# A transformer layer's down-projection in two halves of K, 27 of its 44 weight pieces by seven block products instead of eight

## The chip, the core and the metric

The kernel runs on one core of a Trainium2 chip. A core has a matrix engine (TensorE; PE for its matmuls, PEld for its weight loads), VectorE (DVE), ScalarE (ACT), GpSimd (POOL) and SyncE (SP), each with an instruction queue of its own that runs in order, 16 DMA engines that all queues share, an on-chip memory of 128 partitions and eight accumulation banks of 128 x 512 fp32. The metric is the device time of one execution in microseconds (us).

## What is computed

One layer on 256 tokens of width 2048, all fp32: a mixer (8 attention heads with a forget gate beside 8 HGRN2 heads), cross-attention into 256 memory tokens, and a gated convolutional FFN, each followed by a residual sum and a LayerNorm. The part that the change rewrites is the last product of the FFN:

```python
def conv_ffn(x, w_up, conv_w, conv_b, w_down):
    h = x @ w_up                      # 2048 -> 2 * 5632
    h = causal_depthwise_conv(h, conv_w) + conv_b      # width 3
    a, b = jnp.split(h, 2, axis=-1)
    return (jax.nn.silu(a) * b) @ w_down               # 5632 -> 2048
...
x = layer_norm(DEEPNORM_ALPHA * x + ff, ln3_g, ln3_b)
```

The part that sits early in the program and matters here is `hgrn2_chunkwise`: products of forget gates over ever larger blocks of tokens (prefix products `pre`, suffix products `suf`), which scale queries and keys.

## The kernel before, in words

**Precision.** Every big product splits both operands into a high fp32r part and a low one (`split`, L76: ACT casts the high part, L77; DVE subtracts, L78) and adds three products: high x high, high x low, low x high.

**Weights.** A slot of the program uses one or more loads. A load (`Load`, L88) is one 1 MB DMA of 128 x 2048 fp32 on SP's queue (L99) into one of three `raw` buffers (`RAW_BUFS`), then two `split`s of 128 x 1024 each. `advance` (L154) keeps loads and splits `ahead` loads in front of the slot. All split weights, activations and other work tiles come from one pool of 38 units (`unit`, 4 KB a partition).

**Order of the program.** `run` (L165) walks the slots. In each it pumps one step of the oldest background task (`pump`), runs what was deferred to this slot (`later`), and then the slot's matmuls. Slots of the first 200 us are projections of the mixer (`product_ft`, 16 + 16 matmuls a slot; `product_tok`, 24 a slot). The HGRN2 work (`hgrn`) runs beside them as a background task, twice (g = 0, 1). The instructions of each engine are then put in order by a scheduler, at build time; only dependences on data and the edges that `hold` (L70) draws bind it.

**POOL's part.** For each g `hgrn` has POOL set a quarter of `suf` to one (L463) and clear `AT` (L495). DVE reads that quarter in the reciprocal of L484, and writes into `AT` by a predicated copy in L508. `forget_weights` clears two `ffw` tiles on POOL (L615), into which ACT and DVE put the forget gate's weights (L77, L78). Later POOL issues three DMAs (L657, L660) through a scratch in DRAM, and does five of the splits ahead of the up-projection.

**Down-projection.** `block_output(aps["down"], 11, gT, ...)` (L1081): four blocks of 512 columns, for each 11 pieces of 512 rows of K. A piece is a slot: for both halves t of the tokens, four K steps of three 128 x 512 matmuls (`tok_steps`, L266 to L268), 24 in all. The last four pieces run in one slot, token half by token half, so that the first half's LayerNorm lies under the second half's matmuls. It begins after the whole up-projection, whose gated result stays in 22 tiles `gT`.

## Time and profile before

| | |
|---|---|
| time, median of 3 runs | 1578.58 us (1578.27 to 4043.96) |
| the profiled execution's own time | 1578.25 us |
| its span | 1576.5 us |
| PE busy | 1560.5 us, 99% of the span |
| PEld, DVE, ACT, POOL busy | 85%, 65%, 49%, 1% |
| DMA | 299.29 MB, 190 GB/s over the span |
| down-projection's matmuls | 1324.2 to 1563.6 us, 1056 of 128 x 512 |

Times in the rows are us from the span's start unless marked ns. A matmul's own duration (390 ns) is longer than the distance from one to the next, since they are pipelined. PEld overlaps PE. A view by stretches gives each engine's busy time (with its count of instructions), the granted TensorE clock as a share of full speed, the mean busy share of the 16 DMA engines and the bytes that they moved per second. In the rows "<-" names what is read, behind what is written; in brackets or behind a bar stands the idle time ahead of an instruction and what ended it.

### The profile page before, as it was taken

The page shows a single profiled execution, that of the slowest core. Times are in us where ns is not written, and L with a number is a line of the kernel's source. Part 1 is how long each engine was busy: PE and PEld are TensorE (multiplying, and loading weights), DVE is VectorE, ACT ScalarE, POOL GpSimd, SP SyncE. Part 2 cuts the span into 40 slices and gives each one's busy share as a digit, 9 for nine tenths or more (in the row PEclk, how much of TensorE's full clock was granted, in tenths as well). Part 3 has the DMA queues.
Part 4 walks back from the last instruction along what each step waited for, and adds up shares of the span by engine and source line. Part 5 has one row for each costly group of instructions (what it writes and reads, how often), then busy time and mean ns, then how long its engine had stood idle before and what let it go on. Part 6 is the DMA issues. An engine that isn't in the chain of part 4 may idle for free.

```text
span 1576.5 us, 20804 instructions
## 1 busy us (share of the span) xinstructions
PE 1560.5 (99%) x8324; PEld 1347.3 (85%) x8324; DVE 1025.7 (65%) x1444; ACT 772.2 (49%) x1128; POOL 10.9 (1%) x24
## 2 busy tenths in 40 slices
PE   9999999999999999999999999999999999999996
PEld 7888888888888888988889888888888888888885
DVE  6567468667764775555747976776777777454464
ACT  5453354455553344444617655565555556433340
POOL 0000000000000000000000000000000000000000
PEclk9999999999999999999999999999999999999998
DMA  8565255455445545444733754544454456556551
GB/s 308 193 231 223 109 197 183 175 226 195 155 186 215 212 162 185 161 161 173 271 144 121 275 195 186 214 187 168 180 187 172 176 187 224 202 188 215 195 204 54
DMA packets 45793, 299.29 MB, mean 190 GB/s; under 512 B 5368, under 2 KB 5760, under 8 KB 11264
## 3 DMA queue, kind: packets, MB, share of 16 engines
q1 hardware_dynamic: 45376, 296.90, 51.1%
q8 instruction: 65, 1.06, 0.3%
q0 software_dynamic: 320, 1.06, 0.2%
q14 instruction: 32, 0.26, 0.0%
HBM read 295.83 MB, written 2.11 MB: 189 GB/s over the span
## 4 chain that ended last, share of the span: by engine, by line
PE 98%; DVE 1%; DMA 0%; issue 0%; SPq 0%; DVEq 0%; ACT 0%
PE acc L204 35%; PE acc L206 18%; PE acc L266 13%; PE acc L267 13%; PE acc L268 13%; PE xs L913 1%; PE xo L943 1%; PE lev L536 1%; PE acc L215 0%; PE acc L222 0%; DMA xraw<-in_xT_dram 0%; PE ntr L848 0%; PE fo L760 0%; PE ffacc L623 0%; PE lev L502 0%; PE ho L578 0%
## 5 line engine op out<-in xcount | busy, mean ns | idle before, releaser
L78 DVE TENSOR_TENSOR wlo<-raw,whi 128x1024 fp32r<-128x1024 f32 (+1 forms) x540 | 642.3, 1213 | 262.9 <-ACT whi L77 229.4
L77 ACT CAST whi<-raw 128x1024 fp32r<-128x1024 f32 (+1 forms) x540 | 547.5, 1044 | 277.0 <-PE acc L267 180.9
L204 PE MATMUL acc<-act,whi 128*128 128x512 f32 x2384 | 572.9, 392 | 1.8 <-DVE act L78 1.6
L204 PEld LDWEIGHTS acc<-act,whi 128*128 128x128 f32 x2384 | 438.3, 188 | 87.9 <-DVE act L78 2.0
L206 PEld LDWEIGHTS acc<-act,wlo 128*128 128x128 f32 x2384 | 307.3, 192 | 12.3
L266 PE MATMUL acc<-whi,act 128*128 128x512 f32 x800 | 312.7, 391 | 0.0
L268 PE MATMUL acc<-whi,act 128*128 128x512 f32 x800 | 311.4, 389 | 0.0
L267 PE MATMUL acc<-wlo,act 128*128 128x512 f32 x800 | 311.3, 389 | 0.0
L206 PE MATMUL acc<-act,wlo 128*128 128x256 f32 x2384 | 310.9, 283 | 0.0
L268 PEld LDWEIGHTS acc<-whi,act 128*128 128x128 f32 x800 | 150.2, 188 | 31.4
L266 PEld LDWEIGHTS acc<-whi,act 128*128 128x128 f32 x800 | 150.2, 188 | 30.6
L267 PEld LDWEIGHTS acc<-wlo,act 128*128 128x128 f32 x800 | 150.2, 188 | 30.4
L226 ACT COPY half<-acc 128x256 f32<-128x256 f32 x144 | 53.5, 371 | 144.9 <-PE acc L206 139.4
L959 ACT ACTIVATE cy<-hbuf,convp 128x256 f32<-128x256 f32 x88 | 52.8, 600 | 39.3 <-DVE hbuf L227 39.3
L960 DVE SCALAR_TENSOR_TENSOR cy<-hbuf,convp,cy 128x256 f32<-128x256 f32 x88 | 42.3, 482 | 26.5 <-ACT cy L959 26.5
L77 ACT CAST act<-cy 128x256 fp32r<-128x256 f32 x76 | 30.8, 406 | 57.8 <-DVE cy L978 37.6
L227 DVE TENSOR_TENSOR hbuf<-acc,half 128x256 f32<-128x256 f32 x88 | 36.9, 421 | 29.0 <-ACT half L226 28.3
L266 PE MATMUL acc<-whi,mixT 128*128 128x512 f32 x128 | 50.0, 390 | 0.0
L268 PE MATMUL acc<-whi,mixT 128*128 128x512 f32 x128 | 49.8, 389 | 0.0
L267 PE MATMUL acc<-wlo,mixT 128*128 128x512 f32 x128 | 49.8, 389 | 0.0
L770 DVE SCALAR_TENSOR_TENSOR res<-res,acc 128x512 f32<-128x512 f32 x24 | 16.4, 685 | 48.2 <-PE acc L268 48.2
L78 DVE TENSOR_TENSOR act<-cy,act 128x256 fp32r<-128x256 f32 x76 | 32.0, 422 | 18.7 <-ACT act L77 18.5
(204 smaller groups left out, 723.2 us busy)
## 6 DMA issues: line engine op xcount, KB each, us to landing
raw<-in_up_dram SPq DMA_DIRECT2D x88, 1024.0 KB, 4.8
raw<-in_down_dram SPq DMA_DIRECT2D x44, 1024.0 KB, 4.8
raw<-in_w_ws_dram SPq DMA_DIRECT2D x29, 1024.0 KB, 4.9
raw<-in_w_xs_dram SPq DMA_DIRECT2D x24, 1024.0 KB, 4.9
raw<-in_xk_dram SPq DMA_DIRECT2D x16, 1024.0 KB, 4.9
raw<-in_w_out_dram SPq DMA_DIRECT2D x16, 1024.0 KB, 4.9
raw<-in_xv_dram SPq DMA_DIRECT2D x16, 1024.0 KB, 4.8
raw<-in_xq_dram SPq DMA_DIRECT2D x16, 1024.0 KB, 4.8
```

The costliest lines, as they stand in the source:

```text
L77: nc.scalar.copy(hi, src)
L78: engine.tensor_tensor(lo, src, hi.bitcast(F32), op=ALU.subtract)
L204: nc.tensor.matmul(acc, lhsT=hi, rhs=flat(x), start=k == 0, stop=False)
L206: nc.tensor.matmul(acc[:, 0:S], lhsT=lo, rhs=x[:, 0], start=False, stop=k == KD - 1)
L226: nc.scalar.copy(half, acc[:, S:2 * S])
L227: nc.vector.tensor_tensor(dst, acc[:, 0:S], half, op=ALU.add)
L266: nc.tensor.matmul(acc[t], lhsT=x[:, 0, ts], rhs=hi[:, cols], start=first and j == 0, stop=False)
L267: nc.tensor.matmul(acc[t], lhsT=x[:, 0, ts], rhs=lo[:, cols], start=False, stop=False)
L268: nc.tensor.matmul(acc[t], lhsT=x[:, 1, ts], rhs=hi[:, cols], start=False, stop=last and j == 3)
L770: nc.vector.scalar_tensor_tensor(z, in0=z, scalar=ALPHA, in1=acc, op0=ALU.mult, op1=ALU.add)
L959: nc.scalar.activation(y, h[:, 2:S + 2], AF.Identity, bias=convp[:, 3, f:f + 1], scale=convp[:, 2, f:f + 1])
L960: nc.vector.scalar_tensor_tensor(y, in0=h[:, 1:S + 1], scalar=convp[:, 1, f:f + 1], in1=y, op0=ALU.mult, op1=ALU.add)
```

## The change

**Two halves.** The first 22 feature blocks of the up-projection are followed by the down-projection of their half of K, then comes the second half of both. Each half of the down-projection is 2 x 11 pieces: 2 blocks of 1024 columns, 11 pieces of 256 rows of K. A piece is still 1 MB, now as four blocks of 128 x 512, and still one slot or part of the last one.

**Seven products.** For 27 of the 44 pieces (6 and 6 in the first half, 8 and 7 in the second) the eight block products (2 token halves x 2 K steps x 2 column blocks, three matmuls each) become seven, after Strassen (Winograd's form). Such a piece reads three of its four blocks (768 KB) and a second load of four sums of its blocks (1 MB), and uses four sums of activation blocks, made by `gate_sums` on DVE and split (14 pairs of feature blocks). Its products go to seven accumulators, four of which are combined by `early` after the last such piece of a group of 11; the others take the remaining pieces' eight products too.

**Weight sums.** The four sums of a piece are made in DRAM by six DMAs on POOL's queue (`weight_sums`): a copy of one block to two places, an adding DMA of 128 x 1024 on both, and twice a copy of 128 x 512 and an adding DMA on it. 27 pieces need 162 DMAs, listed in groups of four pieces, step by step. `make_sums` takes one of them off the list in each slot from 72 on, behind a copy of one column on DVE and one on POOL (`marks`).

**Elsewhere.** `ahead` is 2 through the whole up-projection (it was 1 from f = 34 on and in the down-projection).

```diff
+HALVES = 2
+PAIRS = NF // 2 // HALVES
+SEVEN = ((6, 6), (8, 7))
+
+SUMS_FROM = 72
...
+        def __init__(self, src, into=None, cols=2048):
...
+            if self.cols % 1024:
+                w = unit([P, 2, 512], F32R, name="wone")
+                split(w[:, 0], w[:, 1], self.raw[:, 0:512])
+                self.halves.append((w[:, 0], w[:, 1]))
+            for c in range(self.cols % 1024, self.cols, 1024):
                 hi = unit([P, 1024], F32R, name="whi")
                 lo = unit([P, 1024], F32R, name="wlo")
-                split(hi, lo, self.raw[:, h * 1024:(h + 1) * 1024])
+                split(hi, lo, self.raw[:, c:c + 1024])
                 self.halves.append((hi, lo))
+
...
+    class LaterLoad(Load):
+        def dma(self, pieces=1):
+            self.src = self.src()
+            super().dma(pieces)
...
+                make_sums(mine[0].halves[0][0][:, 0:1].bitcast(F32))
                 body(*[m.halves for m in mine])
...
+    def weight_sums(keys, src):
+        def ops(key):
+            w = src(key)
+            t = dp.tile([P, 2048], F32, name=f"wsum{len(made)}")
+            made[key] = t
+            pool = nc.gpsimd
+            yield lambda: pool.dma_start(r3(t[:, 0:1024], 2), w[:, 0:512].unsqueeze(1).broadcast_to((P, 2, 512)))
+            yield lambda: pool.dma_start(t[:, 0:1024], w[:, 512:1536], accum_op=ALU.add)
+            yield lambda: pool.dma_start(t[:, 1024:1536], t[:, 512:1024])
+            yield lambda: pool.dma_start(t[:, 1024:1536], w[:, 512:1024], accum_op=ALU.add)
+            yield lambda: pool.dma_start(t[:, 1536:2048], t[:, 1024:1536])
+            yield lambda: pool.dma_start(t[:, 1536:2048], w[:, 1536:2048], accum_op=ALU.add)
+        for i in range(0, len(keys), 4):
+            for step in zip(*[list(ops(k)) for k in keys[i:i + 4]]):
+                sums_to_make.extend(step)
+    def make_sums(seen):
+        if sums_to_make and state["slot"] >= SUMS_FROM:
+            i = len(sums_to_make) % 8
+            nc.vector.tensor_copy(marks[:, i:i + 1], seen)
+            nc.gpsimd.tensor_copy(marks[:, 8 + i:9 + i], marks[:, i:i + 1])
+            sums_to_make.pop(0)()
+    def three(acc, x, w, start, stop):
+        nc.tensor.matmul(acc, lhsT=x[0], rhs=w[0], start=start, stop=False)
+        nc.tensor.matmul(acc, lhsT=x[0], rhs=w[1], start=False, stop=False)
+        nc.tensor.matmul(acc, lhsT=x[1], rhs=w[0], start=False, stop=stop)
...
+    def columns_1024(pieces, sums, act, act_sums, seven, evac_early, evac, stagger):
+        rest = [i for i in range(len(pieces)) if i not in seven]
+        order, free = [], len(rest) - stagger
+        for n, i in enumerate(seven):
+            order += [i] + rest[n * free // len(seven):(n + 1) * free // len(seven)]
+        order += rest[free:]
+        one, two = {}, {}
+        def into(d, key, tag):
+            start = key not in d
+            if start:
+                d[key] = bank("acc", tag)
+            return d[key], start
+        def seven_body(i):
+            def body(ws, ts):
+                w11, (w22, w21) = ws[0], (block_of(ws[1], 0), block_of(ws[1], 1))
+                (t1, t3), (t2, t4) = ([block_of(t, j) for j in range(2)] for t in ts)
+                x, s = act[i], [(act_sums[i][:, 0, j], act_sums[i][:, 1, j]) for j in range(4)]
+                stop = i == seven[-1]
+                for key, a, b in ((1, x_of(x, 0, 0), w11), (5, s[0], t1), (6, s[1], t2), (7, s[2], t3)):
+                    acc, start = into(one, key, "m")
+                    three(acc, a, b, start, stop)
+                for key, a, b in ((2, x_of(x, 0, 1), w21), (3, s[3], w22), (4, x_of(x, 1, 1), t4)):
+                    acc, start = into(two, key, "g")
+                    three(acc, a, b, start, False)
+            return body
+        def eight(ws, i, t, h, stop):
+            acc, start = into(two, ((2, 3), (4, 8))[t][h], "g")
+            for kk in range(2):
+                three(acc, x_of(act[i], t, kk), block_of(ws[kk], 1 - h), start and kk == 0, stop and kk == 1)
+        def eight_body(i):
+            def body(ws):
+                for t in range(2):
+                    for h in range(2):
+                        eight(ws, i, t, h, False)
+            return body
+        def last_body(*wss):
+            ends = order[-stagger:]
+            for t in range(2):
+                for h in range(2):
+                    for i, ws in zip(ends, wss):
+                        eight(ws, i, t, h, i == ends[-1])
+                    evac(t, h, two[((2, 3), (4, 8))[t][h]])
+        for i in order[:-stagger]:
+            if i in seven:
+                slot([Load(pieces[i][:, 512:2048], cols=1536), LaterLoad(sums[i])], seven_body(i),
+                     (lambda: evac_early(one)) if i == seven[-1] else None)
+            else:
+                slot([pieces[i]], eight_body(i))
+        slot([pieces[i] for i in order[-stagger:]], last_body)
...
     def ffn_b(f):
         def done(y):
+            p = f // 2
             if f % 2 == 0:
                 gT.append(unit([P, 2, 2, S], F32R, name="act"))
-            nc.vector.tensor_tensor(y, gate[f], y, op=ALU.mult)
-            split(gT[f // 2][:, f % 2, 0], gT[f // 2][:, f % 2, 1], y)
+                if p % PAIRS < max(SEVEN[p // PAIRS]):
+                    gated[p] = unit([P, 4, S], name="gated")
+            if p in gated:
+                z = gated[p][:, f % 2]
+            else:
+                z = y
+            nc.vector.tensor_tensor(z, gate[f], y, op=ALU.mult)
+            split(gT[p][:, f % 2, 0], gT[p][:, f % 2, 1], z)
+            if p in gated and f % 2:
+                later(lambda: gate_sums(p))
         return lambda acc: conv(NF + f, acc, done)
+
+    def gate_sums(p):
+        x = gated[p]
+        s = x[:, 2:4].rearrange("p a (b c) -> p (a b) c", b=2)
+        x11, x21, x12, x22 = (x[:, k, t * P:t * P + P] for k in range(2) for t in range(2))
+        for o, a, b, op in ((0, x21, x22, ALU.subtract), (2, x11, x21, ALU.subtract),
+                            (1, s[:, 0], x11, ALU.subtract), (3, x12, s[:, 1], ALU.add)):
+            nc.vector.tensor_tensor(s[:, o], a, b, op=op)
+        gS[p] = unit([P, 2, 4, P], F32R, name="sums")
+        split(gS[p][:, 0], gS[p][:, 1], s)
...
-    set_ahead(2)
-    for f in range(1, NF):
-        if f > 1:
-            product_ft(aps["up"][f], x2T, ffn_a(f))
-        product_ft(aps["up"][NF + f], x2T, ffn_b(f))
-        if f == 34:
-            set_ahead(1)
-    set_ahead(1)
...
-    block_output(aps["down"], 11, gT, n3, 2, after=final, stagger=4)
...
+            columns_1024([down_piece((half, g, p)) for p in range(PAIRS)],
+                         [lambda key=(half, g, p): made[key] for p in range(PAIRS)],
+                         Part(gT, half * PAIRS), Part(gS, half * PAIRS), list(range(SEVEN[half][g])), early, evac,
+                         4 if half and g else 2)
+            if half and g == 0:
+                then(lambda: load_gb(n3, 2))
+    for half in range(HALVES):
+        first, end = half * 2 * PAIRS, (half + 1) * 2 * PAIRS
+        set_ahead(2)
+        for f in range(max(1, first), end):
+            if f > 1:
+                product_ft(aps["up"][f], x2T, ffn_a(f))
+            product_ft(aps["up"][NF + f], x2T, ffn_b(f))
+        down(half)
+    weight_sums([(half, g, p) for half in range(HALVES) for g in range(2) for p in range(SEVEN[half][g])], down_piece)
```

**POOL's queue.** Before, from the first memsets to its end (`suf`, `AT` are HGRN2's tiles, `ffw` the forget gate's):

```order
L362 MEMSET hbuf_83 128x2
L463 MEMSET suf 128x256
L495 MEMSET AT 128x1024
L615 MEMSET ffw 128x1024 x2
L463 MEMSET suf 128x256
L495 MEMSET AT 128x1024
L657 DMA cscr<-ffc 8x256
L660 DMA ncb<-cscr 128x1024 x2
```

After the change, around the first `suf` (104 DMAs of the sums stand between `hbuf_84` and this memset, those of the first four groups and eight of the fifth; `wsum_91` to `wsum_117` are the 27 pieces' sums):

```order
L339 DMA wsum_110<-in_down_dram 128x2x512
L340 DMA wsum_107<-in_down_dram 128x1024
L340 DMA wsum_108<-in_down_dram 128x1024
L340 DMA wsum_109<-in_down_dram 128x1024
L340 DMA wsum_110<-in_down_dram 128x1024
L591 MEMSET suf 128x256
L341 DMA wsum_107<-wsum_107 128x512
```

The memset of `suf`, second in that list before, is now behind 104 DMAs. The first `AT` (L623) is behind 128 of them in the same way. After the change, from the last of the 162 DMAs on:

```order
L344 DMA wsum_117<-in_down_dram 128x512
L743 MEMSET ffw 128x1024 x2
L591 MEMSET suf 128x256
L623 MEMSET AT 128x1024
L785 DMA cscr<-ffc 8x256
L788 DMA ncb<-cscr 128x1024 x2
L355 COPY marks<-marks 128x1 x61
L86 ISA
L86 TENSOR_TENSOR act<-xf,act 128x2x128 x5
L355 COPY marks<-marks 128x1 x101
```

All 162 DMAs stand ahead of the `ffw` memsets, and the 162 copies of `marks` behind them, apart from the DMAs.

**DVE's queue** where the first half of HGRN2 reads `suf`, after the change, with the semaphores that each row waits for:

```order
L86 TENSOR_TENSOR wlo_1043<-raw_927,whi_1042 128x1024 [waits Activation_49]
L247 TENSOR_TENSOR hz_923<-acc_1000,half_1033 128x256 [waits Activation_49]
L612 RECIPROCAL dq_1046<-suf_989 128x64x4 [waits DVE_49,Pool_49]
L86 TENSOR_TENSOR wlo_1088<-raw_978,whi_1087 128x1024 [waits DMAHW4_49,Activation_49]
L86 TENSOR_TENSOR wlo_1092<-raw_978,whi_1091 128x1024 [waits Activation_49]
```

These rows stand where they stood before (there as L484 for the reciprocal and L78 for the weights' low parts): the reciprocal waits for POOL, and the next weights' low parts are behind it.

**SP's queue** at the first half of the down-projection, after the change (before, the 88 loads of `up` were followed by the 44 of `down`):

```order
L107 DMA raw<-in_up_dram 128x2048 x27
L107 DMA raw<-in_down_dram 128x1536
L107 DMA raw<-wsum_91 128x2048
L107 DMA raw<-in_down_dram 128x1536
L107 DMA raw<-wsum_92 128x2048
L107 DMA raw<-in_down_dram 128x2048
L107 DMA raw<-in_down_dram 128x1536
```

Each piece by seven products has two rows, one of them 1536 columns wide; in the second half eight and then seven such pairs follow each other without a 2048-column piece between them.

## Rows read from the trace of the kernel before

**Rows 1.** The page's first part: busy us (share of the span) and instructions.

```profile
PE 1560.5 (99%) x8324; PEld 1347.3 (85%) x8324; DVE 1025.7 (65%) x1444; ACT 772.2 (49%) x1128; POOL 10.9 (1%) x24
```

**Rows 2.** The chain of work that ended last, by engine.

```profile
PE 98%; DVE 1%; DMA 0%; issue 0%; SPq 0%; DVEq 0%; ACT 0%
```

**Rows 3.** The timeline: the down-projection's first matmul and its last.

```profile
1324.21 0.40 PE L266 MATMUL acc<-whi,act 128*128 128x512 f32 x1
...
1563.37 0.39 PE L268 MATMUL acc<-whi,act 128*128 128x512 f32 x1
```

**Rows 4.** The page's groups: splits of 128x1024 on DVE and ACT.

```profile
L78 DVE TENSOR_TENSOR wlo<-raw,whi 128x1024 fp32r<-128x1024 f32 (+1 forms) x540 | 642.3, 1213 | 262.9 <-ACT whi L77 229.4
L77 ACT CAST whi<-raw 128x1024 fp32r<-128x1024 f32 (+1 forms) x540 | 547.5, 1044 | 277.0 <-PE acc L267 180.9
```

**Rows 5.** POOL's timeline: start, us, instruction, idle before and what ended it.

```profile
90.45 0.55 POOL L463 MEMSET suf<- 128x256 f32 x1 [89.35 <-PE acc L268]
121.33 0.96 POOL L495 MEMSET AT<- 128x1024 f32 x1 [30.33 <-PE acc L204]
...
174.20 0.95 POOL L615 MEMSET ffw<- 128x1024 f32 x1 [0.17 <-PE acc L267]
...
376.71 0.69 POOL L657 DMA_DIRECT2D cscr<-ffc  x1 [116.77 <-DVE ffc L655]
379.60 1.09 POOL L660 DMA_DIRECT2D ncb<-cscr  x2 [2.20 <-DMA cscr<-ffc]
```

**Rows 6.** Who reads what POOL set: timeline of DVE, instructions on `ffw`.

```profile
115.31 1.74 DVE L484 RECIPROCAL dq<-suf 128x256 f32<-128x256 f32 x1
116.97 1.16 DVE L78 TENSOR_TENSOR wlo<-raw,whi 128x1024 fp32r<-128x1024 f32 x1
...
142.90 0.73 DVE L508 COPY_PREDICATED AT<-masks,lev 128x512 f32<-128x512 uint8 x1
...
L77 ACT CAST ffw<-ffraw x2: 255/259/263, 196.2 to 196.9; 128x64 fp32r<-128x64 f32 x2
```

**Rows 7.** By stretches (PE, PEld, DVE, ACT, POOL busy; clock, DMA share, GB/s).

```profile
0.00:115.30 115.30, 112.49 (x561) 94.10 (x562) 66.36 (x86) 62.16 (x81) 1.12 (x11) 0.99 0.67 245
115.30:142.90 27.60, 27.60 (x167) 24.64 (x166) 26.65 (x30) 14.31 (x18) 0.96 (x1) 1.00 0.65 233
142.90:196.20 53.30, 53.30 (x285) 45.28 (x284) 24.86 (x31) 16.19 (x20) 1.91 (x2) 1.00 0.36 138
...
1324.20:1563.60 239.40, 239.40 (x1058) 198.03 (x1056) 120.25 (x122) 87.69 (x87) 0.00 (x0) 1.00 0.52 189
1563.60:1576.50 12.90, 0.15 (x1) 0.00 (x0) 8.54 (x20) 0.00 (x0) 0.00 (x0) 0.67 0.23 82
```

**Rows 8.** The page's DMA queues: packets, MB, share of 16 engines' span.

```profile
q1 hardware_dynamic: 45376, 296.90, 51.1%
```

**Rows 9.** Two busy stretches of 20 us, columns as in rows 7.

```profile
20.00:40.00 20.00, 20.00 (x114) 17.49 (x113) 13.13 (x21) 10.60 (x16) 0.00 (x0) 1.00 0.86 311
40.00:60.00 20.00, 20.00 (x112) 17.52 (x111) 15.65 (x16) 12.12 (x15) 0.00 (x0) 1.00 0.85 323
```

**Rows 10.** The page's DMA issues: count, KB each, median us to landing.

```profile
raw<-in_down_dram SPq DMA_DIRECT2D x44, 1024.0 KB, 4.8
...
ncb<-cscr POOLq DMA_DIRECT2D x2, 512.0 KB, 4.6
...
cscr<-ffc POOLq DMA_DIRECT2D x1, 8.0 KB, 2.3
```

**Rows 11.** Small DVE work, and the stretch 1200 to 1300 us (columns as in rows 7).

```profile
L592 DVE SCALAR_TENSOR_TENSOR hy<-hy,hry,hg 128x128 f32<-128x128 f32 x16 | 4.4, 346 | 0.1
172.99 0.17 DVE L559 TENSOR_TENSOR tot<-tot 128x16 f32<-128x16 f32 x1
1200.00:1300.00 100.00, 100.00 (x576) 88.37 (x576) 71.34 (x105) 55.64 (x87) 0.00 (x0) 1.00 0.50 179
```

**Rows 12.** Timeline of PE near the start: groups of four matmuls.

```profile
9.22 1.91 PE L204 MATMUL acc<-act,whi 128*128 128x512 f32 x4
...
13.08 1.09 PE L204 MATMUL acc<-act,whi 128*128 128x512 f32 x4
```

More of the change, by code (lines that the diff above doesn't have):

```diff
@@ L948, in attend, with __init__, __getitem__ @@
         yield
+    class Part:
+        def __init__(self, of, first):
+            self.of, self.first = of, first
+        def __getitem__(self, i):
+            return self.of[self.first + i]
     gT, gate = [], {}
+    gS, gated = {}, {}
     def conv(f, acc, done):
@@ L1079, in final, with down_piece, down, z_of @@
             nc.sync.dma_start(out[t * P:(t + 1) * P, c * 512:(c + 1) * 512], res[:, t, c * 512:(c + 1) * 512])
-    block_output(aps["down"], 11, gT, n3, 2, after=final, stagger=4)
+    def down_piece(key):
+        half, g, p = key
+        return aps["down"][(2 * half + g) * PAIRS + p]
+    def down(half):
+        if half:
+            n3["gb"], n3["params"] = [], [None, None]
+        for g in range(2):
+            def z_of(t, h, g=g):
+                return res[:, t, (2 * g + h) * 512:(2 * g + h + 1) * 512]
+            def early(b, z=z_of):
+                def add(t, h, x, op=ALU.add):
+                    y = z(t, h)
+                    nc.vector.scalar_tensor_tensor(y, in0=y, scalar=1.0 if half else ALPHA, in1=x,
+                                                   op0=ALU.mult, op1=op)
+                def add_more(t, h, x, op):
+                    nc.vector.tensor_tensor(z(t, h), z(t, h), x, op=op)
+                u = unit([P, 2, 512], name="usum")
+                nc.scalar.copy(u[:, 0], b[1])
+                add(0, 0, b[1])
+                add(0, 1, b[5])
+                add(1, 1, b[5])
+                nc.vector.tensor_tensor(u[:, 0], u[:, 0], b[6], op=ALU.add)
+                nc.vector.tensor_tensor(u[:, 1], u[:, 0], b[7], op=ALU.add)
+                add_more(0, 1, u[:, 0], ALU.subtract)
+                add(1, 0, u[:, 1])
+                add_more(1, 1, u[:, 1], ALU.subtract)
+            def evac(t, h, acc, g=g, z=z_of):
+                y = z(t, h)
+                nc.vector.tensor_tensor(y, y, acc, op=ALU.add)
+                if half:
+                    nc.vector.bn_stats(stats[t][:, 2 * g + h], y)
+                    if g == 1 and h == 1:
+                        n3["params"][t] = norm_params(t)
+                        final(t)
+            columns_1024([down_piece((half, g, p)) for p in range(PAIRS)],
[4 more added lines that the diff above has]
+                then(lambda: load_gb(n3, 2))
```

31 lines of the change are left out of this document (20 added, 11 removed).

## The prediction

> **What bounds the kernel now.** I read the page's first part and the chain first: PE is busy 99% of the span and makes 98% of the chain that ended last [rows 1, 2]. So the time is the count of matmuls times their distance, as long as nothing starves PE. The down-projection is the pure case: from its first matmul to its last, 1563.37 - 1324.21 = 239.2 us for 1056 matmuls, thus 226.7 ns from one to the next [rows 3], with PE busy without a gap [rows 7]. DVE and ACT, which make the split weights, have idle time; the DMA engines are half busy over the span. I then looked at what shares a queue with the new work, and that is POOL: 1% busy, with single memsets far apart [rows 1, 5].
>
> **The matmuls saved.** A piece by eight products has 8 x 3 = 24 matmuls, by seven 21. 27 pieces save 81 matmuls of 226.7 ns [rows 3]: -18.4 us. Nothing else leaves PE's path; the tail behind the last matmul (one sum, statistics, LayerNorm and stores, 12.9 us [rows 7]) keeps its form.
>
> **What the seven products cost beside PE.** Such a piece loads 768 KB and 1 MB, 1.835 MB in the 21 x 226.7 ns = 4.76 us that PE needs: 385 GB/s. What the DMA engines can move I take from the whole span: 296.90 MB in 51.1% of 16 engines' 1576.5 us is 368.5 GB/s at full use [rows 8]; two dense stretches say the same, 311 / 0.86 and 323 / 0.85, so 362 and 380 [rows 9]. At 368.5 the piece takes 4.98 us, 0.22 more than PE. In the second half 15 of them follow each other nearly without an ordinary piece between: +3.3 us. The three `raw` buffers, each held from issue over landing (4.8 us [rows 10]) to the end of its splits, could make it more; I take +4 and allow 0 to 15. In the first half an ordinary piece follows two of seven, 4.72 MB in 15.0 us, 315 GB/s, which fits. The extra splits (3.5 pairs of 128 x 1024 a piece instead of 2) are 3.5 x 1.213 = 4.25 us of DVE and 3.65 of ACT [rows 4], under PE's 4.76; without that cover the 27 x 1.5 x 1.213 = 49 us of DVE would show.
>
> **Other work off the path.** `gate_sums` is 14 times four 128 x 128 operations (346 ns is the nearest row [rows 11]) and a split, some 2.1 us, thus 29 us of DVE, and the marks are 162 copies of one column at about 0.17 us [rows 11], 28 us, spread over 162 slots. Both lie in stretches where DVE is about 71% busy [rows 11] behind a full PE: nothing, and at most 57 us if DVE had no slack. `early` replaces other sums into `res`: nothing.
>
> **The DMAs of the weight sums.** This is the large term. `make_sums` issues them from slot 72 on, but between the marks and a DMA there is no dependence, and the build put all 162 at the front of POOL's queue, ahead of the memsets of `suf`, `AT` and `ffw`. POOL's queue does wait for a DMA in order: before, `ncb` stood 2.20 us until `cscr` had landed [rows 5]. So the memset of `suf` comes after 104 DMAs have been issued, the last of them behind landed ones, `AT` after 128, `ffw` after 162. Behind that: DVE reads `suf` at 115.3 us, and the next weights' low parts stand right behind that reciprocal on DVE [rows 6]; then PE has nothing to multiply. `AT` is wanted at 142.9, `ffw` by ACT at 196.2 [rows 6], and the high parts of the weights are queued behind that cast. Before, `suf` was set at 90.45, 25 us ahead of need [rows 5, 6].
>
> When are they issued? A piece's six DMAs write 2 x 512 KB and 4 x 256 KB, 2.10 MB; 27 pieces 56.6 MB, half of it by adding DMAs. Up to 196.2 us the kernel itself moves 245 x 115.3 + 233 x 27.6 + 138 x 53.3 = 42.0 MB [rows 7]. All share the 16 engines, so the end of the sums and the kernel's arrival at `ffw` come together at (42.0 MB + sums) / 368.5 GB/s, whoever goes first:
> - an adding DMA priced as a copy: 98.6 MB, 267.6 us, 71 us later than 196.2;
> - priced twice, because it fetches its destination as well as its source: 42.0 + 28.3 + 2 x 28.3 = 126.9 MB, 344.4 us, +148;
> - priced three times: 155.2 MB, 421 us, +225.
>
> No row of before shows an adding DMA or one from DRAM to DRAM; the nearest are loads of 1 MB in 4.8 us and POOL's two of 512 KB in 4.6 [rows 10]. I take twice: the loads' rate counts one fetch for a byte written, and an addition cannot do with fewer than two. The chain of six steps does not ask for more: four pieces are in flight, and 6 x 4.6 us x 7 groups = 193 us is less than 344. The same sum at `suf` (28.2 MB loaded, 35.7 MB of sums, 16.8 of it counted again) gives 219 us, 104 late; at `AT` 270, 127 late. So the loss comes in three stalls, of about 104, 23 and 21 us, all before 350 us.
>
> The Trainium skill (DMA: Bandwidth & Descriptors, "Issuing engines are not separate DMA queues") states that DMAs started by different engines run on the same 16 DMA engines and interleave, which speaks against a change that adds 56.6 MB beside loads; no run of before shows both queues loaded. Its section "Where 436 GB/s comes from" gives 435 GB/s as the ceiling; 126.9 MB would then end at 292 us, an estimate by that page, and the kernel at 1663 us. The trace's 368.5 [rows 8] decides for me.
>
> **Restarts.** Near the start four matmuls took 1.91 us, and 1.09 a little later [rows 12]; after each of three stalls PE runs a few such groups: +3 us.
>
> **Sum.** The profiled execution's own time is 1578.25 us (span 1576.5, 1.75 around it), 0.3 below the median. 1578.25 - 18.4 + 4 + 148 + 3 = 1715 us.
>
> **Rivals.**
> - *Additions cost no more than copies.* For it: the rate of an engine might be set by what it writes. 1578.25 - 18.4 + 4 + 71 + 3 = 1638 us.
> - *The sums go slower still*: each addition three passes, or runs of 2 KB dearer than the loads' 8 KB (the two loads of 512 KB took almost as long as 1 MB [rows 10]), or four pieces in flight don't fill the engines. Three times gives 1578.25 - 18.4 + 4 + 225 + 3 = 1792; if no two DMAs overlapped, 162 x 3.5 us (between 2.3 and 4.6 [rows 10]) = 567 us, +371, 1938 us.
> - *The sums are hidden (the other side).* If 104 DMAs were through before DVE asks for `suf`, POOL would hold up nobody, and the time would be 1578.25 - 18.4 + 4 = 1564 us, 0.9% below. That decides at 115.3 us: 28.2 + 35.7 = 63.9 MB by then, 554 GB/s, half as much again as 368.5. Transfers that never touch the on-chip memory might run faster than any row shows; against it, the loads' own 28.2 MB already took 67% of the engines in that stretch [rows 7]. The same time comes out if the DMAs left POOL where the source has them, in slots from 72 on; the built order speaks against that.
> - *The down-projection at the limit of the loads*: +15 instead of +4; it moves the sum, not the side.
>
> **Chances.** Additions about twice (1670 to 1760): 0.46. As copies (1610 to 1670): 0.20. Slower still (above 1760): 0.25. Hidden, or nearly: 0.09. The predicted time is the likeliest case, 1715 us. The range 1630 to 1840 leaves out the hidden case and the far end of the slow one, some 0.2 together; it reaches from copies at 380 GB/s (259.5 us, 8 below the 1638) to additions three times with the slow loads and some more. By over 2% (about what a measurement of this kernel can tell from no change) slower means above 1610, faster below 1547: slower 0.90, within 2% 0.09, faster 0.01, since even the hidden case saves 0.9%.
>
> **What would show it.** POOL's timeline begins with DMAs from the first us, and `suf` is set far after 90, near 219; DVE's reciprocal behind it has an idle time of tens of us with POOL as its releaser, then the predicated copy into `AT` and ACT's cast into `ffw`. PE has gaps only before 350 us, the DMA share there is near full, and the bytes per second are well above 245. Two adding DMAs beside two copies of the same size tell the price of an addition. From the end of the stalls on, the sequence is as before; the down-projection's two parts sum to 975 matmuls at 226.7 ns plus a few us. I am wrong if `suf` is set before its reader comes, if the DMAs stand elsewhere in POOL's queue, or if PE's gaps lie in the down-projection.

## The result, and the profile after

| | before | after |
|---|---|---|
| time, median of four runs | 1578.8 us | 1783.55 us (1776.88 to 1784.78) |
| ratio of the times, with its 95% interval | 1 | 1.129 (1.1255 to 1.1325) |
| profiled execution, span | 1576.5 us | 1780.3 us |
| matmuls | 8324 | 8243 |
| PE busy share of the span | 99% | 88% |

One of the four runs before took 4043.96 us and is left out of the ratio.

The kernel became slower by 12.9%; 1715 us was predicted, in a range from 1630 to 1840. The side and the mechanism were right, and the size was some 69 us short: the time lies above 1760 us, where the prediction had its rival "the sums go slower still" with a chance of 0.25, and not between 1670 and 1760, its likeliest case.

The page's first part and the chain of work that ended last, of the kernel after, answer to [rows 1, 2]:

```profile
PE 1570.5 (88%) x8243; PEld 1344.8 (76%) x8243; DVE 1127.5 (63%) x1770; ACT 820.6 (46%) x1200; POOL 185.1 (10%) x348
PE 67%; DMA 23%; DVE 4%; issue 3%; POOL 2%; ACT 1%; DVEq 0%; ACTq 0%; POOLq 0%
```

PE has 81 matmuls fewer and is yet busy 10 us longer: its mean granted clock is 0.940 instead of 0.996, and the matmuls of L224 (L204 before) took 397 ns on average instead of 392. The chain holds 23% of DMA, where it held none. Where in the span that is, the stretches show (PE, PEld, DVE, ACT, POOL busy in us with counts; PE's granted clock, share of the 16 DMA engines, GB/s):

```profile
0.00:20.00 20.00, 10.06 (x28) 5.45 (x28) 4.15 (x6) 4.99 (x7) 6.08 (x17) 0.76 0.88 238
20.00:60.00 40.00, 24.69 (x104) 19.94 (x105) 13.37 (x17) 12.96 (x19) 8.41 (x13) 0.73 0.99 268
...
115.00:160.00 45.00, 45.00 (x230) 38.52 (x229) 24.55 (x33) 23.19 (x28) 12.19 (x18) 1.00 1.03 303
...
200.00:250.00 50.00, 0.00 (x0) 0.00 (x0) 0.00 (x0) 0.00 (x0) 17.94 (x26) 0.50 0.93 172
...
350.00:409.00 59.00, 26.94 (x161) 23.47 (x160) 3.74 (x4) 5.62 (x9) 19.07 (x27) 0.75 0.87 190
409.00:1033.00 624.00, 620.61 (x3276) 534.68 (x3277) 410.57 (x648) 294.72 (x446) 19.36 (x67) 0.99 0.52 189
1286.20:1398.40 112.20, 111.83 (x494) 92.26 (x493) 89.41 (x115) 65.08 (x72) 10.76 (x20) 1.00 0.79 289
1643.30:1764.50 121.20, 115.09 (x485) 88.55 (x483) 96.97 (x118) 63.41 (x73) 0.00 (x0) 1.00 0.75 269
```

The loss lies ahead of 409 us. Between 200 and 250 us no engine but POOL does anything, while the DMA engines are 93% busy. From 409 us on PE is full again, but for the second half of the down-projection: the last two rows are the two halves, and in the second PE is busy 115.09 of 121.20 us. POOL's timeline shows the order that the prediction built on, and answers to [rows 5] (start, us, instruction, idle before and what ended it):

```profile
261.22 0.81 POOL L340 DMA_DIRECT2D wsum<-in_down_dram  x1 [1.39 <-DMA wsum<-in_down_dram]
261.75 0.84 POOL L591 MEMSET suf<- 128x256 f32 x1
...
320.32 0.81 POOL L340 DMA_DIRECT2D wsum<-in_down_dram  x1 [0.27 <-DMA wsum<-in_down_dram]
320.85 1.24 POOL L623 MEMSET AT<- 128x1024 f32 x1
...
406.06 1.73 POOL L344 DMA_DIRECT2D wsum<-in_down_dram  x2 [0.76 <-DMA wsum<-wsum]
407.51 2.14 POOL L743 MEMSET ffw<- 128x1024 f32 x2
```

`suf` was set at 90.45 us and is now set at 261.75, behind 104 DMAs. The waits of the whole span name who stood behind it (engine, line, what it waited for; us in all, times, longest):

```profile
ACT whi L85 <- DMA raw<-in_w_xs_dram: 141.4, 15, 104.1
...
DVE dq L612 <- POOL suf L591: 105.4, 1, 105.4
...
PE acc L226 <- DVE wlo L86: 99.8, 2, 99.3
...
PE acc L224 <- ACT whi L85: 53.9, 10, 34.8
...
ACT ffw L85 <- POOL ffw L743: 44.2, 2, 44.0
...
DVE AT L636 <- POOL AT L623: 30.7, 1, 30.7
...
PE lev L664 <- DVE hq L650: 19.2, 1, 19.2
```

One reciprocal on DVE waits 105.4 us for the memset of `suf`, the low parts of the weights stand behind it on DVE, and PE waits 99.3 us at a stretch for one of them. `AT` holds DVE another 30.7 us and `ffw` ACT 44.0, and PE stands 19.2 and 34.8 us behind them. ACT's 104.1 us for a load belong to the same stall: SP's queue, which issues that load, waits 105.4 us for DVE to finish the splits that free its buffer.

Not all of the delay is a wait for POOL. The last matmuls of L224 ahead of PE's long stop, before and after:

```profile
124.83 3.82 PE L204 MATMUL acc<-act,whi 128*128 128x512 f32 x16
```

```profile
162.32 3.92 PE L224 MATMUL acc<-act,whi 128*128 128x512 f32 x16 [0.34 <-ACT whi L85]
```

PE is 37.5 us late by then, and none of the three memsets has made it wait yet: its weights came late beside the sums.

In sum, from the traces: the transposes of the norm ahead of the up-projection (L976; L848 before), called the norm transposes below, begin at 1033.5 us instead of 826.5, 207.0 later. 37.5 of these us are the late loads, and 169.5 came with the three waits for POOL and the restarts behind them. The down-projection then gives 18.4 us back, and loses 0.7 in its first half, 11.7 in its second and 2.9 in the tail. 207.0 - 18.4 + 0.7 + 11.7 + 2.9 = 203.9, and the spans differ by 203.8.

### The profile page after: what moved, and what is told of

It is laid out like the page before. It is cut to its first block, busy times and chain, and to the rows that moved or that the text cites. A ratio compares the mean times of both kernels' runs of the same rounds, so it can differ in the third digit from the quotient of the medians.

```text
span 1780.3 us, 21576 instructions
## 1 busy us (share of the span) xinstructions
PE 1570.5 (88%) x8243; PEld 1344.8 (76%) x8243; DVE 1127.5 (63%) x1770; ACT 820.6 (46%) x1200; POOL 185.1 (10%) x348
## 3 DMA queue, kind: packets, MB, share of 16 engines
q1 hardware_dynamic: 49264, 318.14, 48.6%
q0 software_dynamic: 20192, 57.69, 16.0%
## 4 chain that ended last, share of the span: by engine, by line
PE 67%; DMA 23%; DVE 4%; issue 3%; POOL 2%; ACT 1%; DVEq 0%; ACTq 0%; POOLq 0%
PE acc L224 27%; DMA wsum<-in_down_dram 15%; PE acc L226 14%; PE acc L288 6%; PE acc L286 6%; PE acc L287 6%; DMA wsum<-wsum 4%; DMA raw<-in_down_dram 3%; PE acc L361 2%; DVE wlo L86 2%; PE acc L360 2%; PE acc L362 2%; DMA raw<-wsum 1%; ACT whi L85 1%; POOL wsum L339 1%
## 5 line engine op out<-in xcount | busy, mean ns | idle before, releaser
L86 DVE TENSOR_TENSOR wlo<-raw,whi 128x1024 fp32r<-128x1024 f32 (+1 forms) x567 | 673.0, 1213 | 206.4 <-ACT whi L85 182.7
L85 ACT CAST whi<-raw 128x1024 fp32r<-128x1024 f32 (+1 forms) x567 | 573.0, 1043 | 386.3 <-DMA raw<-in_w_xs_dram 141.4
L224 PE MATMUL acc<-act,whi 128*128 128x512 f32 x2384 | 584.2, 397 | 63.8 <-ACT whi L85 53.9
L224 PEld LDWEIGHTS acc<-act,whi 128*128 128x128 f32 x2384 | 444.4, 191 | 155.1 <-ACT whi L85 56.7
L286 PE MATMUL acc<-whi,act 128*128 128x512 f32 x448 | 177.0, 395 | 0.0
L287 PE MATMUL acc<-wlo,act 128*128 128x512 f32 x448 | 175.4, 392 | 0.0
L288 PE MATMUL acc<-whi,act 128*128 128x512 f32 x448 | 175.3, 391 | 0.0
L355 POOL COPY marks<-marks 128x1 f32<-128x1 f32 x162 | 58.5, 373 | 913.3 <-DVE marks L354 913.0
L288 PEld LDWEIGHTS acc<-whi,act 128*128 128x128 f32 x448 | 84.7, 189 | 18.0
L286 PEld LDWEIGHTS acc<-whi,act 128*128 128x128 f32 x448 | 85.0, 190 | 17.0
L287 PEld LDWEIGHTS acc<-wlo,act 128*128 128x128 f32 x448 | 84.9, 189 | 17.1
L361 PE MATMUL acc<-wlo,act 128*128 128x512 f32 x190 | 74.2, 393 | 1.8 <-DVE wlo L86 1.8
L362 PE MATMUL acc<-whi,act 128*128 128x512 f32 x190 | 73.8, 389 | 0.0
L612 DVE RECIPROCAL dq<-suf 128x256 f32<-128x256 f32 x4 | 7.0, 1739 | 105.4 <-POOL suf L591 105.4
L360 PE MATMUL acc<-whi,act 128*128 128x512 f32 x190 | 72.2, 389 | 0.0
```

What stands on the lines that cost most here:

```text
L85: nc.scalar.copy(hi, src)
L86: engine.tensor_tensor(lo, src, hi.bitcast(F32), op=ALU.subtract)
L224: nc.tensor.matmul(acc, lhsT=hi, rhs=flat(x), start=k == 0, stop=False)
L286: nc.tensor.matmul(acc[t], lhsT=x[:, 0, ts], rhs=hi[:, cols], start=first and j == 0, stop=False)
L287: nc.tensor.matmul(acc[t], lhsT=x[:, 0, ts], rhs=lo[:, cols], start=False, stop=False)
L288: nc.tensor.matmul(acc[t], lhsT=x[:, 1, ts], rhs=hi[:, cols], start=False, stop=last and j == 3)
```

## The experiments

The theory after the result: all of the loss is made by the 162 DMAs, by two ways together, the place in POOL's queue and the load on the DMA engines; the seven products themselves save what their count says. The rivals: the load on the engines alone makes it, so that the order on POOL does not matter; or the seven products bring a cost of their own that the delay covers. Spans are compared with 1576.5 us, and a half is measured from its first matmul to its last, against its intervals of 226.7 ns. Where no ratio is given, the time is that of a single execution. The changed kernels' executions lie up to 8 us apart (1776.88 to 1784.78 for the kernel after), so a difference of one or two us between two of their traces is only a hint.

### The DMAs held at their slots

```
-            nc.gpsimd.tensor_copy(marks[:, 8 + i:9 + i], marks[:, i:i + 1])
-            sums_to_make.pop(0)()
+            seen = nc.gpsimd.tensor_copy(marks[:, 8 + i:9 + i], marks[:, i:i + 1])
+            hold(sums_to_make.pop(0)(), seen)
```

> The changed kernel with one edge more: each DMA of the weight sums is held behind its own mark on POOL, so that POOL's queue has suf, AT, ffw and the scratch DMAs first and then a mark, a DMA, a mark, a DMA. Theory A (the loss comes from the memsets that stood behind the DMAs on POOL): the stalls before 410 us vanish, and what is left is the down-projection as the changed kernel shows it, 81 matmuls less (-18.4 us), its two halves 12.4 us longer than their matmuls and its tail 2.9 us longer: 1578.3 - 18.4 + 12.4 + 2.9 = 1575 us, within 6. Theory B (the loss is the DMA engines' time that the sums take, about 280 us of all 16, wherever they stand in the queue): well above 1600 us, with PE waiting for weights somewhere between 450 and 1500 us.

Measured: 1595.1 us, ratio 1.0109 (1.0092 to 1.0126). Each DMA now stands behind its own mark, the first at 440 us (POOL's timeline):

```profile
440.47 0.18 POOL L355 COPY marks<-marks 128x1 f32<-128x1 f32 x1 [59.79 <-DVE marks L354]
440.59 0.74 POOL L339 DMA_DIRECT2D wsum<-in_down_dram  x1
```

`suf` is set at 90.43 us, and the norm transposes begin at 826.6: the 207 us are gone to the last tenth. So the loss came from DMAs that had left the slots where the source has them. But 1575 us was expected, and the kernel is slower than the one before: the halves lost 15.6 and 14.2 us and the tail 2.9. -18.4 + 15.6 + 14.2 + 2.9 = +14.3, and the spans differ by 14.2. At one DMA a slot the 162 last to about 1412 us, so they ran beside the loads of the first half, and these took longer: 5.7 us for 768 KB and 6.2 for 1 MB of sums, after 4.2 and 4.9 in the kernel after.

### The three memsets on DVE, the DMAs still at the front

```
-        hold(nc.gpsimd.memset(s4[:, :, 3], 1.0), ready)
+        hold(nc.vector.memset(s4[:, :, 3], 1.0), ready)
```

The memsets of `AT` and `ffw` are changed alike.

> The changed kernel with the memsets of suf, AT and ffw on DVE instead of POOL; the 162 DMAs stay at the front of POOL's queue and run from the first us. Theory A (memsets late behind the DMAs are the cause, and sharing the engines a smaller part): no DVE or ACT wait for POOL is left; loads that get half of 368 GB/s while they need 245 up to 115 us and 233 up to 143 lose 28.2 MB / 184 GB/s - 115 = 38 and 6.4 / 184 GB/s - 28 = 7 us, so about 1575 + 45 = 1620 us, between 1595 and 1650. Theory B (sharing the engines is all of it): 1750 to 1790 us as in the changed kernel.

Measured: 1683.45 us, between the two expectations; the norm transposes come 101.0 us late. That isn't all the load on the DMA engines, for two of POOL's works stay where they were: the DMAs through the scratch, `cscr` and `ncb`, still stand behind the 162. The matmuls ahead of PE's stop, in the kernel before and then in this one, those behind it, POOL's queue there, and ACT's wait in between:

```profile
393.16 1.89 PE L720 MATMUL s<-fk,fq 128*128 128x256 f32 x8
```

```profile
444.21 1.89 PE L848 MATMUL s<-fk,fq 128*128 128x256 f32 x8
...
487.25 3.78 PE L224 MATMUL acc<-act,whi 128*128 128x512 f32 x8 [39.30 <-ACT whi L85]
```

```profile
478.97 0.83 POOL L785 DMA_DIRECT2D cscr<-ffc  x1
486.71 1.13 POOL L788 DMA_DIRECT2D ncb<-cscr  x2 [6.91 <-DMA cscr<-ffc]
```

```profile
ACT whi L85 <- DMA cscr<-ffc: 51.6, 1, 51.6
```

Before, `cscr` was issued at 376.71 us [rows 5], and ACT had no such wait. So PE was 51.0 us late when it stopped, and the other 50.0 came with 39.3 us of waiting for `cscr` and what follows on `ncb`: POOL's place once more. The 51.0 are what sharing the DMA engines had cost PE by 447 us with no memset late, not far from the 45 that theory A had worked out. What failed is its sign that no wait for POOL would be left. The sums ran on to 486 us; what sharing alone would have added behind 447 us, no run shows. The stretches (columns as above) show the engines full and PE short of weights:

```profile
0.00:60.00 60.00, 34.55 (x128) 24.29 (x129) 16.76 (x23) 17.19 (x25) 13.92 (x29) 0.77 0.96 253
...
115.00:200.00 85.00, 80.60 (x415) 69.04 (x414) 56.61 (x68) 39.78 (x50) 20.89 (x29) 0.98 1.00 302
```

Before, PE was busy for 57.19 of the first 60 us; here it is for 34.55. Loads of `w_ws` and `w_xs` that took 4.9 us (medians) took 8.5 and 9.7 in the kernel after. The Trainium skill (DMA: Bandwidth & Descriptors, "Issuing engines are not separate DMA queues") says that transfers started by different engines share the same 16 engines and interleave; the traces agree: POOL's DMAs nearly doubled the landing time of SP's.

### What an addition costs

```
-            yield lambda: pool.dma_start(t[:, 0:1024], w[:, 512:1536], accum_op=ALU.add)
+            yield lambda: pool.dma_start(t[:, 0:1024], w[:, 512:1536])
```

The two other adding DMAs are changed alike.

> The changed kernel with the three adding DMAs of each piece made plain copies of the same size (the weight sums are left out). Theory A (an adding DMA is priced at 2.6 copies: the trace of the changed kernel has 512 KB additions landing 3.7 us apart where 512 KB copies land 1.4 apart): the DMAs end at (42.0 + 56.6 MB) / 368 GB/s = 268 us instead of 407, so the ffw memset 139 us earlier and the kernel at about 1783 - 139 = 1644 us, within 15. Rival (any transfer from DRAM to DRAM is as dear, adding or not): still 1760 us or more.

Measured: 1715.71 us, again between. The DMA queue of the sums, of the kernel after and then of this one (packets, MB, share of 16 engines' span):

```profile
q0 software_dynamic: 20192, 57.69, 16.0%
```

```profile
q0 software_dynamic: 16736, 57.69, 11.7%
```

As copies the bytes take 11.7% of 1713.7 us, 200.5 us of all 16 engines, so 288 GB/s, where the loads of the kernel after run at 368 (318.14 MB in 48.6% of its span). With additions they take 16.0% of 1780.3, 284.8 us. 56.6 MB of the 57.69 are sums: 28.3 MB of copies take 98 us, 28.3 MB of additions 181, or 156 GB/s. An addition thus costs 1.84 copies of the same kind, and 2.36 loads. The factor of two was nearly right; what it was put on, the loads' rate, was not the rate of these copies. Whether they are slower because both ends lie in DRAM or because their packets are shorter (57.69 MB in 16736 packets here, 318.14 MB in 49264 on the loads' queue) no run separates. Nor is the price a constant: the same 57.69 MB with additions took 272 us of the engines with the memsets on DVE (16.2% of 1681.4) and 296 in the next experiment, which puts the additions between 147 and 167 GB/s if the copies are taken at 288.

### The sums alone, in the kernel before

```
+                make_sums(mine[0].halves[0][0][:, 0:1].bitcast(F32))
...
+    weight_sums(list(range(27)), lambda k: aps["down"][k])
```

with `weight_sums`, `make_sums` and `marks` as in the change; nothing reads the sums.

> The kernel before with nothing changed but the 162 DMAs and their marks added, as the change has them (nothing reads the sums; the down-projection is the old one). Theory A: all of the loss and 207 us of it is there when the up-projection starts, so 1578 + 207 = 1785 us, within 8. Rival (the halves or the seven products take part of it, through units or ahead): clearly less, below 1770 us.

Measured: 1797.67 us, `suf` at 267.83, the norm transposes 219.4 us late, and so the end. The DMAs make the whole loss by themselves, without a single seven-product, and beyond the stalls nothing is lost or won. It came out 4.7 us above the upper end of what was expected (1785 with 8 to either side); the stalls are 12 us longer than after's, and the sums took 296 us of the engines (16.5% of 1795.9) instead of 285. Why they took more is open.

### The DMAs held, from slot 16 on

```
-SUMS_FROM = 72
+SUMS_FROM = 16
```

with the hold of the first experiment.

> All 27 seven-products as in the kernel after, each sum DMA held behind its own mark, and the marks begin at slot 16 instead of 72, so at one DMA a slot the last of 162 comes some 56 slots (about 330 us at 6 us a slot) earlier than the 1412 us of the held kernel: about 1080 us, where the first half of the down-projection begins. Theory A (in the held kernel the first half lost 15.6 us because sum DMAs ran beside the loads of the seven-pieces): that half goes back to 112 to 114 us, the second stays at 121 to 124, the tail at +2.7, nothing is late before: span 1576.5 - 18.4 + 1 + 13 + 2.7 = 1575, so 1577 us. Theory B (the seven-pieces' own splits and loads cost the first half what they cost, sums or not): the half stays near 127 us, 1590 us. Theory C (sums this early delay the loads of the front, where PE already waits): the norm transposes come over 5 us later than 826.5, and the time is 1585 or more.

Measured: 1584.48 us, ratio 1.0045 (1.003 to 1.006). The norm transposes begin at 827.1 us, so sums this early cost the front 0.6 us. The last DMA is issued at 1089 us, and the first half falls from 126.9 to 118.7 us: 8.2 of its 15.6 us went with the sums that ran beside its loads. But 7.4 remain, and 14.3 in the second half. The last sums landed at 1100 us, so that the first 20 us of the half still had some beside them. Three stretches of 10 us of the first half (columns as above):

```profile
1110.00:1120.00 10.00, 9.86 (x44) 7.76 (x43) 5.92 (x7) 4.49 (x6) 0.00 (x0) 1.00 0.90 326
1120.00:1130.00 10.00, 7.84 (x34) 5.92 (x32) 10.00 (x14) 6.58 (x8) 0.00 (x0) 1.00 0.59 212
1130.00:1140.00 10.00, 9.92 (x36) 8.04 (x37) 5.40 (x8) 1.83 (x4) 0.00 (x0) 0.83 0.57 184
```

The DMA engines are at 59%, so it isn't their rate; DVE is busy for 10.00 of the 10 us, and behind it PE runs at 0.83 of its clock. DVE's timeline there:

```profile
1120.61 0.68 DVE L1245 SCALAR_TENSOR_TENSOR res<-res,acc 128x512 f32<-128x512 f32 x1
1121.20 2.36 DVE L86 TENSOR_TENSOR wlo<-raw,whi 128x1024 fp32r<-128x1024 f32 x2
1123.47 1.28 DVE L1245 SCALAR_TENSOR_TENSOR res<-res,acc 128x512 f32<-128x512 f32 x2
1124.67 0.68 DVE L1256 TENSOR_TENSOR usum<-usum,acc 128x512 f32<-128x512 f32 x1
1125.27 1.22 DVE L86 TENSOR_TENSOR wlo<-raw,whi 128x1024 fp32r<-128x1024 f32 x1
1126.41 0.68 DVE L1257 TENSOR_TENSOR usum<-usum,acc 128x512 f32<-128x512 f32 x1
1127.00 0.68 DVE L1249 TENSOR_TENSOR res<-res,usum 128x512 f32<-128x512 f32 x1
```

The operations on `res` and `usum` are `early`, eight of 0.64 to 0.68 us, some 5.2 us. A seven-piece has 4.25 us of splits in PE's 4.76, so DVE has 0.5 us a piece to spare. That gave the theory for the later runs: `early` costs, and the more the denser the seven-products stand.

### `early` left out

```
-                     (lambda: evac_early(one)) if i == seven[-1] else None)
+                     None)
```

with the hold and `SUMS_FROM` at 16.

> All 27 seven-products, sum DMAs held from slot 16, and the eight DVE operations and one ACT copy of `early` (which add the banks of the seven products into `res`) left out, so that part of the output is missing. With them the halves were 118.7 us (492 matmuls, 111.5 at 226.7 ns) and 123.6 us (483, 109.5). Theory A (`early` on a DVE that the splits of the seven-pieces fill to 91% is what stops PE in the first half, the loads in the second): first half 112 to 113, second 115 to 119 us, tail near the 13.1 us of the kernel before: span about 1570 us. Theory B (the loads of the seven-pieces, or their splits, stop PE without `early` too): the halves stay within 1.5 us of 118.7 and 123.6, span 1579 to 1581.

Measured: 1572.54 us, span 1570.8, 12.4 us shorter than with `early`, which is more than the 6.7 us that the four executions with it lie apart (1583.16 to 1589.90). The first half takes 112.2 us, 0.9 over its count: without `early` nearly the whole loss of this half is gone. The same 10 us as above, now of this kernel:

```profile
1120.00:1130.00 10.00, 10.00 (x46) 8.21 (x45) 6.99 (x7) 6.20 (x7) 0.00 (x0) 1.00 0.72 272
```

The second half fell from 123.6 to 119.3, so some 4 of its 14.3 us may be `early`'s, and 10.0 stay; second halves with the same products and `early` lost between 11.7 and 17.7 us in the other kernels, so the split is rough. There the longest waits between 1437 and 1557 us are for loads:

```profile
ACT whi L85 <- DMA raw<-wsum: 25.3, 13, 3.5
...
ACT wone L85 <- DMA raw<-in_down_dram: 8.9, 6, 5.3
...
PE acc L360 <- ACT whi L85: 3.9, 6, 1.2
```

The tail measured 14.5 us from the start of the last matmul, after 16.0 with `early` and 13.1 before. So about half of its 2.9 us hung on `early`, and what makes the other half stays open.

### Four seven-products

```
-SEVEN = ((6, 6), (8, 7))
+SEVEN = ((1, 1), (1, 1))
```

with the hold and `SUMS_FROM` at 72.

> The two halves of K with one seven-product in each of the four column groups (4 instead of 27, 24 sum DMAs, held at their slots from 72 on). What the halving by itself costs. Theory A (nothing but the tail and four pieces' worth): 12 matmuls less at 226.7 ns = -2.7, tail up to +2.7, so 1577 to 1580 us with the two half-projections together within 2 us of 1056 - 12 matmuls. Theory B (the split of K, more evacuations and restarts of the clock after each half cost some us each): 1585 us or more.

Measured: 1575.36 us, span 1573.6, both halves 118.1 us, exactly 521 intervals of 226.7 ns, and the tail 12.9. 12 matmuls fewer are 2.7 us, and the span is 2.9 shorter: two halves of K cost nothing that shows.

### Eighteen seven-products

```
-SEVEN = ((6, 6), (8, 7))
+SEVEN = ((6, 6), (5, 1))
```

with the hold and slot 16.

> 18 seven-products, placed 6 and 6 in the first half and 5 and 1 in the second, sum DMAs held at their slots from slot 16 on. 54 matmuls less = -12.2 us. Theory A (the stalls come where seven-pieces follow each other at over the load rate, and the tail grows because the last column group's seven-products end late): the first half +1, the second +1 to +3 instead of +12, tail +0 to +1 since the last group's only seven-product comes first: 1578.6 - 12.2 + 1 + 2 + 1 = 1570 us, between 1567 and 1574, a ratio of 0.993 to 0.997. Theory B (each seven-product costs as much in waits as it saves): 1576 to 1582 us.

Measured: 1568.31 us, ratio 0.9937 (0.9923 to 0.9951). The second half took its count exactly, 115.4 us, and the tail 13.0; the first half, with its 12 seven-products as they were, still lost 5.0, though here the last of the sums had landed at 772 us. (The profiled execution was the longest of the five, 1571.96 us.) Then the same number, spread more evenly, the rest as in this kernel:

```
-SEVEN = ((6, 6), (8, 7))
+SEVEN = ((5, 5), (5, 3))
```

> The same 18 seven-products with sum DMAs held from slot 16, placed 5 and 5 in the first half and 5 and 3 in the second instead of 6, 6, 5, 1. With 6 a column group ran two seven-pieces in a row; with 5 an ordinary piece stands behind nearly each. With 6, 6 the first half was 116.3 us for 492 matmuls (111.5 at 226.7 ns), 4.8 us over, with DVE busy without a pause in the 10 us in which `early` adds the seven products; with 5, 1 the second was 115.4 us for 510 matmuls (115.6), nothing over. Theory A (what costs is density: splits fill DVE to 91% in a seven-piece, so `early` can only be made up in ordinary pieces): first half 498 matmuls in 113 to 114 us, second 504 in 114.3 to 115.5, time 1566 to 1568 us, ratio 0.992 to 0.993. Theory B (each `early` costs its 2 to 2.5 us whatever stands around it): halves 5 and 4 us over, 1572 us, ratio 0.996.

Measured: 1566.06 us (1565.33 to 1568.03), ratio 0.9918 (0.9904 to 0.9931), against 1578.9 of the kernel before beside it. The first half lost 2.0 us instead of 5.0, the second nothing:

```profile
1079.00:1194.50 115.50, 113.77 (x504) 93.94 (x503) 83.86 (x90) 61.73 (x69) 0.00 (x0) 1.00 0.73 266
1439.00:1553.70 114.70, 114.61 (x507) 94.59 (x506) 86.56 (x107) 50.93 (x57) 0.00 (x0) 1.00 0.63 236
```

54 matmuls are 12.2 us; 2.0 of them were lost, and the span is 10.3 shorter. (Here too the profiled execution was the longest, 1568.03 us.) The time is what the theory by density expected, and not the 1572 us of a fixed price for each `early`; it rests on two placements. This version beats both kernels, the one before by 0.8%: small, but the slowest of its five executions lies 10 us under the fastest of the nine before (1578.61).

## Why the prediction was right, and where it was off

- **The mechanism: right.** The DMAs stood at the front of POOL's queue, `suf`, `AT` and `ffw` were late in that order, DVE's reciprocal and ACT's cast waited for POOL, and all stalls behind POOL lay ahead of 409 us. The hold takes the 207 us away and the sums alone make them: nothing else is needed. One sign that it named did not show: the bytes per second were not well above 245 (172 to 303 in the rows ahead of 409 us). And one of its signs of being wrong showed in part: PE has gaps in the second half of the down-projection too, some 6 us of 121.
- **The DMAs of the sums: the mis-sized term.** 148 us predicted at `ffw`, 212.6 measured (ACT's cast of `ffw` at 408.8 us instead of 196.2). The step that failed is "priced twice" at 368.5 GB/s for every byte: 28.3 MB of copies and 28.3 MB of additions make 230 us by it, and they took 98 + 181 = 279, since a copy from DRAM to DRAM ran at 288 GB/s. That is 49 of the missing 64 us. The other 15 are engines that were not full: the DMA share falls to 0.87 to 0.93 wherever loads have stopped. This is the rival "slower still", by two of the three reasons that it gave, transfers dearer than the loads and engines that are not filled; additions at three passes, its price of 1792 us, come near the measured time by luck, for an addition took 2.36 loads.
- **The single stalls.** 104, 23 and 21 us were predicted, 105.4, 30.7 and 44.0 measured. The first fits by an accident of two errors: `suf` came 42.8 us later than forecast (261.75 instead of 219), but DVE also came to it later. 157.3 us, not 115.3, was when it began to wait. The late loads, which had put PE 37.5 us behind when it stopped, are in the forecast of the sum (all bytes share the engines) but were not told as a delay of their own.
- **The hidden sums.** This rival needed 63.9 MB by 115 us; at that point POOL had issued 38 DMAs, not 104. Its other form, DMAs that stay in their slots, was priced at 1564 us and measured 1595.1: the price left out what the sums do to the loads of the first half, and, as far as the run without it tells, `early`.
- **The matmuls saved: right.** 81 at 226.7 ns; wherever PE did not wait, a half took its count of intervals to 0.1 us.
- **Seven-pieces at the limit of the loads: right place, short size.** +4 was taken with 0 to 15 allowed, and 0.7 + 11.7 were measured. For the second half +3.3 came from 385 against 368.5 GB/s; it lost 11.7 to 17.7 us in the five kernels with all 27 and `early` (17.7 with the memsets on DVE), and 10.0 without `early`. The DMA share in the last one is 0.82 to 0.99 while the seven-pieces run, mostly not full, and SP's queue waits 78.8 us in 31 places for DVE's splits to free a buffer. This points to the three buffers that the prediction spoke of; no run had a fourth, so it isn't shown.
- **"`early` replaces other sums into `res`: nothing": wrong.** Its DVE time comes at one spot, where the splits leave 0.5 us a piece. It hardly showed in the kernel after (0.7 us in the first half), but with the sums held it cost 7.4 - 0.9 = 6.5 us there. The first half of the kernel after, with the same work on DVE, got by with 0.7 (1.7 and 2.5 in the two other kernels that had the sums at the front and these products): its loads landed sooner (medians of 4.2, 4.9 and 5.2 us for 768 KB, 1 MB of sums and 1 MB in the down-projection, against 5.0, 6.3 and 6.9 in the kernel held from slot 16). So `early` alone isn't enough; it costs where the splits are already late. The last sums, which landed 20 us into that half, are a part of it, but not all: the kernel of 18 lost 5.0 there with its sums long landed. What else makes the splits late was not settled.
- **The tail "keeps its form": wrong by 2.9 us**, half of it `early`.
- **Restarts: +3.** They can't be told apart from the stalls; the granted clocks of 0.73 to 0.76 in the stretches ahead of 409 us in which PE works with pauses show them, and the clock was back at 1.00 in the two halves.
- **The other prices.** The marks and the sums of activations cost nothing where DVE has room, as predicted: with the hold, PE lost nothing between 115 and 1079 us. The extra splits cost nothing where ordinary pieces stand between: the second half of the first kernel of 18 took its count.

## What to carry to other kernels

An instruction stays where it is written only if something holds it there: look in the built order for what a scheduler has moved to the front of a queue, and count what stands behind it. Price a transfer by its kind (load, copy between DRAM places, addition) before by its bytes, and ask what else its bytes delay, for 37.5 of this loss of 207 us were loads that came late, and 51 where no memset waited. An experiment that is to take all waits for a queue away has to move everything that others wait for: the scratch DMAs left on POOL made half of the delay in the one with the memsets on DVE. A saving of PE's time is worth only as much as the engines that feed it have left in that same stretch: taking two thirds of the seven-products, evenly spread, won 12.8 us where all of them won none.

## What the runs showed of the hardware

- DMA rates, in GB/s of bytes written over the time that their packets took of all 16 engines: loads 361 to 371 over whole runs, copies from DRAM to DRAM 288 (one run), adding copies 156 (147 to 167). The Trainium skill (DMA: Bandwidth & Descriptors, "Where 436 GB/s comes from") has 435 GB/s as the ceiling, and says that transfers between HBM and SBUF are bound nearer 358 GB/s; the whole runs lie near the second, but it is no bound here: in the first kernel of 18, 10 us of the second half moved 425 GB/s, close to the first. On additions the runs alone speak.

```profile
1492.00:1502.00 10.00, 10.00 (x46) 8.27 (x45) 8.14 (x11) 2.09 (x3) 0.00 (x0) 1.00 1.03 425
```

- With loads stopped, four adding DMAs of 512 KB landed 3.3 to 4.5 us apart. In POOL's timeline of the kernel after, each copy (L341) stands until the addition of its own piece has landed, and POOL's queue with it:

```profile
215.91 0.56 POOL L341 DMA_DIRECT2D wsum<-wsum  x1 [3.58 <-DMA wsum<-in_down_dram]
220.40 0.55 POOL L341 DMA_DIRECT2D wsum<-wsum  x1 [3.93 <-DMA wsum<-in_down_dram]
223.69 0.53 POOL L341 DMA_DIRECT2D wsum<-wsum  x1 [2.74 <-DMA wsum<-in_down_dram]
227.37 0.53 POOL L341 DMA_DIRECT2D wsum<-wsum  x1 [3.15 <-DMA wsum<-in_down_dram]
```

- A wait of PE of about 2 us can cost twice that: in the kernel held from slot 16, PE was idle for 2.2 us between 1120 and 1130 us, and the next 10 us ran at a granted clock of 0.83 with 36 matmuls instead of 46.
